# Attention weights transposed one query tile at a time, and a float32 value product in two column halves

## The chip, the cores and the metric

One core of a Trainium2 chip runs the whole program. The metric is device time in microseconds (us), the median of the runs of one kernel. TensorE (PE) multiplies matrices into PSUM; VectorE (DVE), ScalarE (ACT) and GpSimd (POOL) work on tiles; the DMA queues are fed by SyncE (SP). PEld stands for TensorE's weight loads, which can run beside its matmuls.

## The reference

A block of one layer on a sequence of 2048 rows with 1024 channels: RMS norm, one wide input projection, a state-space branch (SSD), a stick-breaking attention branch with 16 heads of 64 channels, gates, an output projection, and a norm. The part that the change touches is the attention:

```python
for blk in range(L // SB_BLOCK):
    ...
    logits = jnp.einsum('bqhd,bkhd->bhqk', q[:, q0:kend], k[:, :kend]).astype(jnp.float32) * scale
    mask = ki < qi
    log_fail = jnp.where(mask, jax.nn.log_sigmoid(-logits), 0.0)
    between = lax.cumsum(log_fail, axis=3, reverse=True) - log_fail
    w = jnp.where(mask, jnp.exp(jax.nn.log_sigmoid(logits) + between), 0.0)
    outs.append(jnp.einsum('bhqk,bkhd->bqhd', w.astype(v.dtype), v[:, :kend]))
```

## The kernel before, in words

The kernel runs in stages. First come the input projection's columns for the attention and the values (the V stage, `unit_v`), then the SSD branch (about 395 to 910 us), then the attention (about 929 to 2665 us), then the output.

Products with float32 accuracy are written in two ways. Most of them split each operand into a high and a low part of type fp32r, and add two or three fp32r products. Some are plain float32 products; each of these stands as two PE instructions in the trace. In the SSD stage the products `yp` are plain float32, with 64 columns of weights, and go by turns to the lower and the upper 64 partitions of one PSUM tile.

The attention works in steps `(h, qs, kc)`: a head, a block of 512 queries and a block of 512 keys, 160 steps in all. For each head, `qs` goes from 3 down to 0, and `kc` from `qs` down to 0. 64 of the steps are diagonal (`kc == qs`), 96 are not. A step has four query tiles `i` of 128 queries and four key blocks `kb` of 128 keys.

- `attn_qk(s, i)`: two products into `lg` (PE), two sigmoids into `tc` and `sw` (ACT), masks on POOL in diagonal steps, a running product over the keys (the scan, DVE), and the product of `sw` with it (DVE). The result `sw` holds the weights of query tile `i`: queries on partitions, keys along the row.
- `attn_tr(s, kb)`: the weights have to stand with the keys on partitions. For one key block it transposes the blocks of all query tiles `i` into one PSUM tile `wtp` (PE), and splits that into `wh` (ACT) and `wl` (DVE).
- `attn_av(s, kb)`: the product with the values of that key block. `vt` holds the high parts of the values in columns 0 to 63 and the low parts in columns 64 to 127; it is multiplied with `wh` and with `wl`, so `po` has the high parts' sum in one half of its partitions and the low parts' sum in the other, and the two are added at the end of a query block.

PE's order is written out by hand (`chain` ties each matmul to the one before it). The loop of a step goes over `i`: `attn_tr(s, i)`, `attn_qk(s + 1, i)`, `attn_av(s, i - 2)` from `i = 2` on, and `fill(i)`; then two more `attn_av` with a `fill` each. `fill` puts matmuls of other projections (`proj`) between, in shares given by `FW`. The other engines' queues follow the order in which a tile framework schedules the recorded operations.

Of the kernel before, what the change touches and what calls it, by code (L numbers as in the profile page):

```python
# [23 lines left out]
HD = 64  # L24
EPS = 1e-6
WARM = 24
FW = (0.8, 0.9, 1.0, 1.0, 1.1, 1.2)

COL_Z = 0
COL_X = 1024  # L30
# [18 lines left out]
def hybrid_kernel(ctx, tc, x, norm_pre, w_in, b_gate, conv_w, conv_b, dt_bias, a_log, d_skip,  # L49
# [57 lines left out]

    kst = [drp.tile([P, L], F32, name=f"kst{h}") for h in range(HEADS)]
    qst = [drp.tile([P, L], F32, name=f"qst{h}") for h in range(HEADS)]
    vst = [drp.tile([L, 4, P], F32, name=f"vst{i}") for i in range(HEADS // 4)]  # L110
    csd = drp.tile([HEADS, L], F32, name="csd")
    ytd = [drp.tile([D, TB], F32, name=f"ytd{t}") for t in range(NTB)]
    otd = [drp.tile([D, TB], F32, name=f"otd{t}") for t in range(NTB)]
# [272 lines left out]
    with tc.tile_pool(name="va", bufs=2) as va, tc.tile_pool(name="vp", bufs=2, space=PSUM) as vp:  # L386
        kn = va.tile([P, NCH, 16], F32, name="kn", bufs=1)

        def prep_v(i):
            c0, cw = vch[i]  # L390
            vh, vl = [], []
            for k in range(KT):
                raw = va.tile([P, cw], F32, name="vraw", tag="vraw", bufs=4)
                nc.sync.dma_start(raw, w_in[k * P:(k + 1) * P, c0:c0 + cw])
                h = va.tile([P, cw], F32R, name="vhi", tag="vhi", bufs=12)
                nc.scalar.copy(h, raw)
                l = va.tile([P, cw], F32R, name="vlo", tag="vlo", bufs=12)
                nc.vector.tensor_sub(l, raw, h.bitcast(F32))
                vh.append(h)
                vl.append(l)  # L400
            return vh, vl

        def unit_v(i, c, wv):
            c0, cw = vch[i]
            vh, vl = wv
            off = cw - VW
            tb, o = c // CPB, (c % CPB) * P
            ps = vp.tile([P, TB], F32, name="vps", tag="vps", bufs=3)
            for k in range(KT):
                xh, xl = hh[tb][:, k, o:o + P], hl[tb][:, k, o:o + P]  # L410
                matmul(ps[:, :cw], xh, vh[k], start=(k == 0), stop=False)
                yield
                matmul(ps[:, :cw], xh, vl[k], start=False, stop=False)
                yield
                matmul(ps[:, :cw], xl, vh[k], start=False, stop=(k == KT - 1))
                yield
            if off:
                nc.vector.tensor_copy(kn[:, c, :], ps[:, :16])
            v = va.tile([P, 4, 2, HD], F32R, name="vt", tag="vt", bufs=3)
            src = ps[:, off:cw].rearrange("p (h d) -> p h d", d=HD)  # L420
            nc.scalar.copy(v[:, :, 0, :], src)
            nc.vector.tensor_sub(v[:, :, 1, :], src, v[:, :, 0, :].bitcast(F32))
            nc.sync.dma_start(vst[i][c * P:(c + 1) * P], v.bitcast(F32).rearrange("p h s d -> p h (s d)"))

        def last_k():
            knf = kn.rearrange("p c d -> p (c d)")
            kd = kst[HEADS - 1].rearrange("(s d) t -> d s t", s=2)
            for r0 in range(0, NCH * 16, P):
                n = min(P, NCH * 16 - r0)
                tp = vp.tile([P, P], F32, name="ktp", tag="ktp")  # L430
                transpose(tp[:n], knf[:, r0:r0 + n], ident)
                kt = va.tile([P, 2, P], F32R, name="kt", tag="kt")
                nc.scalar.copy(kt[:n, 0, :], tp[:n])
                nc.vector.tensor_sub(kt[:n, 1, :], tp[:n], kt[:n, 0, :].bitcast(F32))
                for c in range(n // 16):
                    t0 = (r0 // 16 + c) * P
                    nc.sync.dma_start(kd[HD - 16:HD, :, t0:t0 + P], kt[c * 16:(c + 1) * 16].bitcast(F32))

        wv = prep_v(0)
        for tb in range(NTB):  # L440
            run(proj(w9, tb, done_qk(ev, 9, tb)))
        for i in range(len(vch)):
            for c in range(NCH):
                if c == max(0, NCH - 6) and i + 1 < len(vch):
                    nxt = prep_v(i + 1)
                run(unit_v(i, c, wv))
            if i == 0:
                later(20, last_k)
            if i + 1 < len(vch):
                wv = nxt  # L450
        wb = prep_a(COL_B)
        flush()
# [326 lines left out]

    steps = [(h, qs, kc) for h in range(HEADS) for qs in reversed(range(NTB)) for kc in reversed(range(qs + 1))]  # L780
    last_head = min(i for i, s in enumerate(steps) if s[0] == HEADS - 1)
    fills = {"gen": fill_h(), "left": n_main, "pos": 6 * last_head, "acc": 0.0, "late": False}

    def tick():
        clock[0] += 1
# [3 lines left out]
    def fill(i):  # L789
        f = fills  # L790
        if f["pos"] <= 0:
            for _ in f["gen"]:
                tick()
            if f["late"]:
                return
            f.update(gen=fill_y(box_y), left=8 * 24, pos=6 * (len(steps) - last_head) - 3, acc=0.0, late=True)
        f["acc"] += f["left"] / f["pos"] * FW[i]
        f["pos"] -= 1
        while f["acc"] >= 1.0:
            f["acc"] -= 1.0  # L800
            f["left"] -= 1
            if next(f["gen"], 0) == 0:
                f["left"] = 0
                break
            tick()
# [3 lines left out]
    def attn_load(s):  # L809
        if s >= len(steps):  # L810
            return
        h, qs, kc = steps[s]
        if (h, qs) not in qts:
            qa = ab.tile([P, TB], F32R, name="qa", tag="qa", bufs=2)
            qb = ab.tile([P, TB], F32R, name="qb", tag="qb", bufs=2)
            cols = slice(qs * TB, (qs + 1) * TB)
            nc.sync.dma_start(qa.bitcast(F32), qst[h][:, cols])
            nc.sync.dma_start(qb[0:HD].bitcast(F32), qst[h][HD:P, cols])
            nc.sync.dma_start(qb[HD:P].bitcast(F32), qst[h][0:HD, cols])
            qts[h, qs] = qa, qb  # L820
        if (h, kc) not in kts:
            k = ab.tile([P, TB], F32R, name="kt", tag="kt", bufs=4)
            nc.sync.dma_start(k.bitcast(F32), kst[h][:, kc * TB:(kc + 1) * TB])
            v = ab.tile([P, CPB, P], F32R, name="vt", tag="vt", bufs=4)
            nc.sync.dma_start(v.bitcast(F32), vst[h // 4][kc * TB:(kc + 1) * TB, h % 4, :].rearrange(
                "(c p) d -> p c d", p=P))
            kts[h, kc], vts[h, kc] = k, v

    def attn_qk(s, i):
# [29 lines left out]

    wts = {}  # L860

    def attn_tr(s, kb):
        h, qs, kc = steps[s]
        q0 = kb if kc == qs else 0
        lo = q0 * P
        tp = ap.tile([P, TB], F32, name="wtp", tag="wtp", bufs=3)
        for i in range(q0, CPB):
            transpose(tp[:, i * P:(i + 1) * P], ws[s, i][:, kb * P:(kb + 1) * P], ident)
        wh = ab.tile([P, TB], F32R, name="wh", tag="wh", bufs=3)
        nc.scalar.copy(wh[:, lo:], tp[:, lo:])  # L870
        wl = ab.tile([P, TB], F32R, name="wl", tag="wl", bufs=3)
        nc.vector.tensor_sub(wl[:, lo:], tp[:, lo:], wh[:, lo:].bitcast(F32))  # L872
        wts[s, kb] = lo, wh, wl

    def attn_av(s, kb):
        h, qs, kc = steps[s]
        lo, wh, wl = wts.pop((s, kb))
        if (h, qs) not in pos:
            pos[h, qs] = ap.tile([P, TB], F32, name="po", tag="po", bufs=1)
        po, v = pos[h, qs], vts[h, kc]  # L880
        first = kc == qs and kb == 0
        final = kc == 0 and kb == CPB - 1
        matmul(po[:, lo:], v[:, kb, :], wh[:, lo:], start=first, stop=False, skip_group_check=True)
        matmul(po[:, lo:], v[:, kb, :], wl[:, lo:], start=False, stop=final, skip_group_check=True)
        if final:
            e0 = (h % 2) * HD
            mine, other = slice(e0, e0 + HD), slice(HD - e0, P - e0)
            z = ab.tile([P, TB], F32, name="zl", tag="zl", bufs=1)
            nc.sync.dma_start(z[mine], zsd[qs][h * HD:(h + 1) * HD, :])
            o = gz.tile([P, TB], F32, name="o", tag="gz", bufs=2)  # L890
            nc.scalar.copy(o[mine], po[other])
            nc.vector.tensor_add(o[mine], o[mine], po[mine])  # L892
            nc.vector.tensor_mul(o[mine], o[mine], z[mine])  # L893
            nc.sync.dma_start(otd[qs][h * HD:(h + 1) * HD, :], o[mine])
# [9 lines left out]
    for s in range(len(steps)):  # L904
        attn_load(s + 2)
        for i in range(CPB):
            attn_tr(s, i)
            attn_qk(s + 1, i)
            if i >= 2:
                attn_av(s, i - 2)  # L910
            fill(i)
        for i in range(2, CPB):
            attn_av(s, i)
            fill(i + 2)
    for _ in fills["gen"]:
        pass
    close_ap()
# [150 lines left out]
```

## Time and profile before

| | |
|---|---|
| median of the runs | 3163.7 us (3163.27 to 3165.02, 3 runs) |
| the profiled execution's own time, its span | 3163.6 us |
| PE busy | 3024.1 us (96%) |
| DVE busy | 2457.2 us (78%) |
| ACT busy | 1585.7 us (50%) |
| POOL busy | 477.9 us (15%) |

The span is that of one profiled execution; nothing else lies around it here, and it agrees with the median. Matmuls are pipelined and their ends are modelled, so start times of neighbouring matmuls tell more than the durations: a 512-column fp32r matmul is shown with 0.39 us, while the next starts 0.23 us after it. An idle time in front of an instruction stands in brackets with what ended it.

### The profile page before, as it was taken

The numbers are of one execution on the slowest core, as the hardware profiler recorded it, in microseconds if no ns is written. First come the engines' busy times: TensorE is split into PE (matmuls) and PEld (weight loads), VectorE is DVE, ScalarE is ACT, GpSimd is POOL, SyncE is SP. The second block draws the span as 40 slices with busy tenths as digits, with TensorE's granted clock in tenths as the row PEclk, the third lists the DMA queues.
The fourth block names the chain that finished last, engine by engine and source line by source line (L and its number), as shares of the span: only waits on it lengthen the run. The fifth ranks groups of instructions, "written<-read, shape, count | busy, mean of one in ns | idle before, by whom it ended". The sixth has DMA issues, their size and how long they took to land.

```text
span 3163.6 us, 48155 instructions
## 1 busy us (share of the span) xinstructions
PE 3024.1 (96%) x16169; PEld 2496.9 (79%) x16169; DVE 2457.2 (78%) x4357; ACT 1585.7 (50%) x3102; POOL 477.9 (15%) x1626
## 2 busy tenths in 40 slices
PE   8999999999999999999999999999999989999998
PEld 6899888787877777777777777777777767888887
DVE  7321688768869989989899999989998899756553
ACT  6211345434446666566565666566665656333321
POOL 0000011100111212122212121222111231101000
PEclk9999999999999999999999999999999999999999
DMA  5532022212243334224323333334233334555452
GB/s 165 148 122 93 24 71 80 68 40 67 72 128 89 90 89 110 80 81 113 93 70 103 94 97 91 87 94 114 69 89 90 111 117 144 176 148 167 133 167 70
DMA packets 298816, 320.63 MB, mean 101 GB/s; under 512 B 23148, under 2 KB 187848, under 8 KB 298568
## 3 DMA queue, kind: packets, MB, share of 16 engines
q1 hardware_dynamic: 298416, 317.51, 34.6%
q8 instruction: 128, 2.10, 0.3%
q14 instruction: 120, 0.98, 0.1%
q10 hardware_dynamic: 152, 0.05, 0.0%
HBM read 216.67 MB, written 100.79 MB: 100 GB/s over the span
## 4 chain that ended last, share of the span: by engine, by line
PE 53%; DVE 33%; issue 5%; DMA 4%; ACT 4%; POOL 1%; SPq 0%; DVEq 0%; POOLq 0%; ACTq 0%
PE proj L74 30%; DVE tc L852 13%; PE po L74 8%; DVE sw L853 7%; PE vps L74 6%; DVE wl L872 5%; PE wtp L77 4%; PE lg L74 3%; DMA csb<-csd 2%; ACT sw L845 1%; ACT wh L870 1%; PE yp L74 1%; DVE acc L474 1%; DVE o L893 1%; DVE o L892 1%
## 5 line engine op out<-in xcount | busy, mean ns | idle before, releaser
L74 PE MATMUL proj<-hh,whi 128*128 128x512 f32 x1920 | 762.0, 397 | 0.1
L74 PE MATMUL proj<-hh,wlo 128*128 128x512 f32 x1920 | 761.7, 397 | 0.0
L74 PE MATMUL proj<-hl,whi 128*128 128x512 f32 x1920 | 760.4, 396 | 1.3 <-DVE hl L286 1.1
L870 ACT CAST wh<-wtp 128x512 fp32r<-128x512 f32 (+3 forms) x640 | 337.1, 527 | 390.2 <-PE wtp L77 386.6
L852 DVE TENSOR_TENSOR_SCAN tc<-tc,cy 128x513 f32<-128x513 f32 x384 | 490.9, 1278 | 0.3 <-ACT tc L843 0.3
L872 DVE TENSOR_TENSOR wl<-wtp,wh 128x512 fp32r<-128x512 f32 (+3 forms) x640 | 383.0, 599 | 81.5 <-ACT wh L870 80.3
L77 PE MATMUL wtp<-ident,sw 128*128 128x128 f32 x2176 | 369.9, 277 | 72.2 <-DVE sw L853 70.1
L853 DVE TENSOR_TENSOR sw<-sw,tc 128x512 f32<-128x512 f32 (+3 forms) x640 | 394.2, 616 | 50.5 <-POOL sw L849 13.5
L77 PEld LDWEIGHTS wtp<-ident,sw 128*128 128x128 f32 x2176 | 280.7, 141 | 181.0 <-DVE sw L853 99.1
L74 PEld LDWEIGHTS proj<-hl,whi 128*128 128x128 f32 x1920 | 362.6, 189 | 72.6 <-DVE hl L286 2.5
L74 PEld LDWEIGHTS proj<-hh,wlo 128*128 128x128 f32 x1920 | 362.6, 189 | 70.7 <-issue 0.3
L74 PEld LDWEIGHTS proj<-hh,whi 128*128 128x128 f32 x1920 | 362.7, 189 | 70.1 <-ACT hh L285 0.5
L845 ACT ACTIVATE sw<-lg 128x512 f32<-128x512 f32 (+3 forms) x640 | 346.1, 541 | 49.8 <-PE wtp L77 49.6
L843 ACT ACTIVATE tc<-lg 128x512 f32<-128x512 f32 (+3 forms) x640 | 349.1, 545 | 18.7 <-PE lg L74 13.1
L132 ACT CAST whi<-wraw 128x512 fp32r<-128x512 f32 x248 | 154.3, 624 | 280.5 <-PE proj L74 178.9
L74 PE MATMUL lg<-kt,qa 128*128 128x512 f32 (+3 forms) x640 | 285.1, 445 | 0.0
L74 PE MATMUL po<-wl,vt 128*128 128x512 f32 (+3 forms) x640 | 242.6, 379 | 29.0 <-DVE wl L872 28.2
L852 DVE TENSOR_TENSOR_SCAN tc<-tc 128x129 f32<-128x129 f32 (+3 forms) x256 | 218.1, 852 | 26.3 <-POOL tc L847 25.2
L74 PE MATMUL lg<-kt,qb 128*128 128x512 f32 (+3 forms) x640 | 234.6, 367 | 0.0
L74 PE MATMUL po<-wh,vt 128*128 128x512 f32 (+3 forms) x640 | 232.4, 363 | 0.0
L134 DVE TENSOR_TENSOR wlo<-wraw,whi 128x512 fp32r<-128x512 f32 x246 | 173.4, 706 | 73.3 <-ACT whi L132 70.5
L856 POOL COPY cy<-tc 128x1 f32<-128x1 f32 x384 | 133.6, 348 | 448.7 <-DVE tc L852 448.7
(202 smaller groups left out, 4887.8 us busy)
## 6 DMA issues: line engine op xcount, KB each, us to landing
wraw<-in_w_in SPq DMA_DIRECT2D x120, 256.0 KB, 3.0
vst<-vt SPq DMA_DIRECT2D x64, 256.0 KB, 2.0
csb<-csd SPq DMA_DIRECT2D x64, 256.0 KB, 4.4
qa<-qst SPq DMA_DIRECT2D x64, 256.0 KB, 3.5
qb<-qst SPq DMA_DIRECT2D x128, 128.0 KB, 3.8
kt<-kst SPq DMA_DIRECT2D x64, 256.0 KB, 3.2
vt<-vst SPq DMA_DIRECT2D x64, 256.0 KB, 3.0
gtd<-zb SPq DMA_DIRECT2D x64, 256.0 KB, 2.1
```

The lines of the kernel that those rows point to most:

```text
L74: chain(nc.tensor.matmul(*a, **k))
L77: chain(nc.tensor.transpose(*a))
L132: nc.scalar.copy(h, raw)
L134: (eng or nc.vector).tensor_tensor(l, raw, h.bitcast(F32), op=ALU.subtract)
L474: nc.vector.scalar_tensor_tensor(acc, xp[:, i:i + TB], pv[:, col:col + 1], acc, op0=ALU.mult, op1=ALU.add)
L843: nc.scalar.activation(t[:, :W], lg[:, :W], AF.Sigmoid, scale=-0.125)
L845: nc.scalar.activation(w[:, :W], lg[:, :W], AF.Sigmoid, scale=0.125)
L852: nc.vector.tensor_tensor_scan(tr, tr, tr, 1.0 if diag else carry[h, qs, i], ALU.mult, ALU.min)
L853: nc.vector.tensor_mul(w[:, :W], w[:, :W], t[:, 1:W + 1])
L856: nc.gpsimd.tensor_copy(c, t[:, 0:1])
L870: nc.scalar.copy(wh[:, lo:], tp[:, lo:])
L872: nc.vector.tensor_sub(wl[:, lo:], tp[:, lo:], wh[:, lo:].bitcast(F32))
```

## The change

`attn_tr` now takes a query tile `i` in place of a key block. It transposes that tile's four key blocks, and ACT copies them, undivided, as float32 into a buffer `wt` of the whole step (two such buffers). In a diagonal step only the blocks up to the diagonal are transposed, and POOL writes zeros into the one further block that the value product reads. `wl`, the DVE instruction for it, and the split of the values are gone: `vt` holds float32 values with 64 columns for each key block, in another layout in DRAM. `attn_av` works on a whole step: four plain float32 products with 64 columns of weights, the key blocks going by turns to the lower and the upper 64 partitions of `po`. It is issued once a step, for the step before (`attn_av(s - 1)`, after `attn_qk(s + 1, 1)` and `fill(1)`). `fill` has five places for a step in place of six.

```diff
--- before.py
+++ after.py
@@ -24,7 +24,7 @@
 HD = 64
 EPS = 1e-6
 WARM = 24
-FW = (0.8, 0.9, 1.0, 1.0, 1.1, 1.2)
+FW = (1.0, 1.0, 1.2, 1.2, 0.6)
 
 COL_Z = 0
 COL_X = 1024
@@ -107,7 +107,7 @@
 
     kst = [drp.tile([P, L], F32, name=f"kst{h}") for h in range(HEADS)]
     qst = [drp.tile([P, L], F32, name=f"qst{h}") for h in range(HEADS)]
-    vst = [drp.tile([L, 4, P], F32, name=f"vst{i}") for i in range(HEADS // 4)]
+    vst = [drp.tile([P, 4, NCH, HD], F32, name=f"vst{i}") for i in range(HEADS // 4)]
     csd = drp.tile([HEADS, L], F32, name="csd")
     ytd = [drp.tile([D, TB], F32, name=f"ytd{t}") for t in range(NTB)]
     otd = [drp.tile([D, TB], F32, name=f"otd{t}") for t in range(NTB)]
@@ -416,11 +416,9 @@
                 yield
             if off:
                 nc.vector.tensor_copy(kn[:, c, :], ps[:, :16])
-            v = va.tile([P, 4, 2, HD], F32R, name="vt", tag="vt", bufs=3)
-            src = ps[:, off:cw].rearrange("p (h d) -> p h d", d=HD)
-            nc.scalar.copy(v[:, :, 0, :], src)
-            nc.vector.tensor_sub(v[:, :, 1, :], src, v[:, :, 0, :].bitcast(F32))
-            nc.sync.dma_start(vst[i][c * P:(c + 1) * P], v.bitcast(F32).rearrange("p h s d -> p h (s d)"))
+            v = va.tile([P, 4, HD], F32, name="vt", tag="vt", bufs=3)
+            nc.scalar.copy(v, ps[:, off:cw].rearrange("p (h d) -> p h d", d=HD))
+            nc.sync.dma_start(vst[i][:, :, c, :], v)
 
         def last_k():
             knf = kn.rearrange("p c d -> p (c d)")
@@ -779,7 +777,7 @@
 
     steps = [(h, qs, kc) for h in range(HEADS) for qs in reversed(range(NTB)) for kc in reversed(range(qs + 1))]
     last_head = min(i for i, s in enumerate(steps) if s[0] == HEADS - 1)
-    fills = {"gen": fill_h(), "left": n_main, "pos": 6 * last_head, "acc": 0.0, "late": False}
+    fills = {"gen": fill_h(), "left": n_main, "pos": len(FW) * last_head, "acc": 0.0, "late": False}
 
     def tick():
         clock[0] += 1
@@ -793,7 +791,7 @@
                 tick()
             if f["late"]:
                 return
-            f.update(gen=fill_y(box_y), left=8 * 24, pos=6 * (len(steps) - last_head) - 3, acc=0.0, late=True)
+            f.update(gen=fill_y(box_y), left=8 * 24, pos=len(FW) * (len(steps) - last_head) - 3, acc=0.0, late=True)
         f["acc"] += f["left"] / f["pos"] * FW[i]
         f["pos"] -= 1
         while f["acc"] >= 1.0:
@@ -821,9 +819,8 @@
         if (h, kc) not in kts:
             k = ab.tile([P, TB], F32R, name="kt", tag="kt", bufs=4)
             nc.sync.dma_start(k.bitcast(F32), kst[h][:, kc * TB:(kc + 1) * TB])
-            v = ab.tile([P, CPB, P], F32R, name="vt", tag="vt", bufs=4)
-            nc.sync.dma_start(v.bitcast(F32), vst[h // 4][kc * TB:(kc + 1) * TB, h % 4, :].rearrange(
-                "(c p) d -> p c d", p=P))
+            v = ab.tile([P, CPB, HD], F32, name="vt", tag="vt", bufs=4)
+            nc.sync.dma_start(v, vst[h // 4][:, h % 4, kc * CPB:(kc + 1) * CPB, :])
             kts[h, kc], vts[h, kc] = k, v
 
     def attn_qk(s, i):
@@ -859,30 +856,31 @@
 
     wts = {}
 
-    def attn_tr(s, kb):
+    def attn_tr(s, i):
         h, qs, kc = steps[s]
-        q0 = kb if kc == qs else 0
-        lo = q0 * P
+        n = i + 1 if kc == qs else CPB
         tp = ap.tile([P, TB], F32, name="wtp", tag="wtp", bufs=3)
-        for i in range(q0, CPB):
-            transpose(tp[:, i * P:(i + 1) * P], ws[s, i][:, kb * P:(kb + 1) * P], ident)
-        wh = ab.tile([P, TB], F32R, name="wh", tag="wh", bufs=3)
-        nc.scalar.copy(wh[:, lo:], tp[:, lo:])
-        wl = ab.tile([P, TB], F32R, name="wl", tag="wl", bufs=3)
-        nc.vector.tensor_sub(wl[:, lo:], tp[:, lo:], wh[:, lo:].bitcast(F32))
-        wts[s, kb] = lo, wh, wl
-
-    def attn_av(s, kb):
+        sw = ws.pop((s, i))
+        for kb in range(n):
+            transpose(tp[:, kb * P:(kb + 1) * P], sw[:, kb * P:(kb + 1) * P], ident)
+        if i == 0:
+            wts[s] = ab.tile([P, CPB, TB], F32, name="wt", tag="wt", bufs=2)
+            if kc == qs:
+                nc.gpsimd.memset(wts[s][:, 1, 0:P], 0.0)
+        nc.scalar.copy(wts[s][:, 0:n, i * P:(i + 1) * P], tp[:, 0:n * P].rearrange("p (k q) -> p k q", q=P))
+
+    def attn_av(s):
         h, qs, kc = steps[s]
-        lo, wh, wl = wts.pop((s, kb))
         if (h, qs) not in pos:
             pos[h, qs] = ap.tile([P, TB], F32, name="po", tag="po", bufs=1)
         po, v = pos[h, qs], vts[h, kc]
-        first = kc == qs and kb == 0
-        final = kc == 0 and kb == CPB - 1
-        matmul(po[:, lo:], v[:, kb, :], wh[:, lo:], start=first, stop=False, skip_group_check=True)
-        matmul(po[:, lo:], v[:, kb, :], wl[:, lo:], start=False, stop=final, skip_group_check=True)
-        if final:
+        wt = wts.pop(s)
+        for kb in range(CPB):
+            lo = kb * P if kc == qs and kb > 1 else 0
+            e = (kb % 2) * HD
+            matmul(po[e:e + HD, lo:], v[:, kb, :], wt[:, kb, lo:], start=(kc == qs and kb < 2),
+                   stop=(kc == 0 and kb >= 2), skip_group_check=True)
+        if kc == 0:
             e0 = (h % 2) * HD
             mine, other = slice(e0, e0 + HD), slice(HD - e0, P - e0)
             z = ab.tile([P, TB], F32, name="zl", tag="zl", bufs=1)
@@ -906,12 +904,11 @@
         for i in range(CPB):
             attn_tr(s, i)
             attn_qk(s + 1, i)
-            if i >= 2:
-                attn_av(s, i - 2)
             fill(i)
-        for i in range(2, CPB):
-            attn_av(s, i)
-            fill(i + 2)
+            if i == 1 and s > 0:
+                attn_av(s - 1)
+                fill(CPB)
+    attn_av(len(steps) - 1)
     for _ in fills["gen"]:
         pass
     close_ap()
```

Three places in the program show what moves. The names are those of the tiles: `wtp` the transposed weights, `lg` the logits, `po` the value product, `proj` the filling projections; a trailing count stands for so many equal rows.

PE in the step in front of a diagonal one, before, from the transposes of key block 2 to those of key block 3:

```order
L77 MATMUL wtp<-ident,sw 128x128 x4
L74 MATMUL lg<-kt,qa 128x384
L74 MATMUL lg<-kt,qb 128x384
L74 MATMUL po<-wh,vt 128x512
L74 MATMUL po<-wl,vt 128x512
L74 MATMUL proj<-hh_195,wlo 128x512
L74 MATMUL proj<-hh_195,whi 128x512
L74 MATMUL proj<-hl_199,whi 128x512
L74 MATMUL proj<-hh_195,wlo 128x512
L77 MATMUL wtp<-ident,sw 128x128 x4
L74 MATMUL lg<-kt,qa 128x512
L74 MATMUL lg<-kt,qb 128x512
```

The same place in the changed kernel, from the transposes of query tile 1 to those of query tile 2:

```order
L77 MATMUL wtp<-ident,sw 128x128 x4
L74 MATMUL lg<-kt,qa 128x256
L74 MATMUL lg<-kt,qb 128x256
L74 MATMUL proj<-hh_197,whi 128x512
L74 MATMUL proj<-hl_201,whi 128x512
L74 MATMUL proj<-hh_197,wlo 128x512
L74 MATMUL proj<-hh_197,whi 128x512
L74 MATMUL po<-wt,vt 64x512 x4
L74 MATMUL proj<-hl_201,whi 128x512
L74 MATMUL proj<-hh_197,wlo 128x512
L74 MATMUL proj<-hh_197,whi 128x512
L77 MATMUL wtp<-ident,sw 128x128 x4
```

Before, a pair of `po` products with 512 columns follows each of the later `lg` pairs. Now four `po` products with 64 columns of weights stand together, once, behind the `proj` matmuls of the second query tile.

PE in a diagonal step, before; the rows start with the value product of key block 0:

```order
L74 MATMUL po<-wh,vt 128x512
L74 MATMUL po<-wl,vt 128x512
L74 MATMUL proj<-hh_196,whi 128x512
L74 MATMUL proj<-hl_200,whi 128x512
L74 MATMUL proj<-hh_196,wlo 128x512
L74 MATMUL proj<-hh_196,whi 128x512
L77 MATMUL wtp<-ident,sw 128x128
L74 MATMUL lg<-kt,qa 128x512
L74 MATMUL lg<-kt,qb 128x512
L74 MATMUL po<-wh,vt 128x384
L74 MATMUL po<-wl,vt 128x384
L74 MATMUL proj<-hl_200,whi 128x512
```

The value product of a diagonal step in the changed kernel (it stands inside the step after it), with its neighbours:

```order
L74 MATMUL proj<-hh_196,wlo 128x512
L74 MATMUL proj<-hh_196,whi 128x512
L74 MATMUL proj<-hl_200,whi 128x512
L74 MATMUL proj<-hh_196,wlo 128x512
L74 MATMUL po<-wt,vt 64x512 x2
L74 MATMUL po<-wt,vt 64x256
L74 MATMUL po<-wt,vt 64x128
L74 MATMUL proj<-hh_196,whi 128x512
L74 MATMUL proj<-hl_200,whi 128x512
L74 MATMUL proj<-hh_196,wlo 128x512
```

Before, four pairs with 512, 384, 256 and 128 columns are spread over the step. Now there are four products in a row, with 512, 512, 256 and 128 columns.

DVE at the same place, before; SCALAR_TENSOR_TENSOR with 129 to 513 columns is the scan:

```order
L852 SCALAR_TENSOR_TENSOR tc<-tc 128x129
L853 TENSOR_TENSOR sw<-sw,tc 128x128
L872 TENSOR_TENSOR wl<-wtp,wh 128x512
L852 SCALAR_TENSOR_TENSOR tc<-tc 128x257
L853 TENSOR_TENSOR sw<-sw,tc 128x256
L872 TENSOR_TENSOR wl<-wtp,wh 128x512
L852 SCALAR_TENSOR_TENSOR tc<-tc 128x385
L853 TENSOR_TENSOR sw<-sw,tc 128x384
L872 TENSOR_TENSOR wl<-wtp,wh 128x512
L852 SCALAR_TENSOR_TENSOR tc<-tc 128x513
```

DVE at the same place in the changed kernel:

```order
L849 SCALAR_TENSOR_TENSOR tc<-tc 128x129
L850 TENSOR_TENSOR sw<-sw,tc 128x128
L849 SCALAR_TENSOR_TENSOR tc<-tc 128x257
L850 TENSOR_TENSOR sw<-sw,tc 128x256
L849 SCALAR_TENSOR_TENSOR tc<-tc 128x385
L850 TENSOR_TENSOR sw<-sw,tc 128x384
L849 SCALAR_TENSOR_TENSOR tc<-tc 128x513
L850 TENSOR_TENSOR sw<-sw,tc 128x512
```

The `wl` rows between the scan and the product of one query tile and those of the next are gone; the rest keeps its order.

## Rows read from the trace of the kernel before

**Rows 1.** The page's first part: busy us (share of the span) and instructions.

```profile
PE 3024.1 (96%) x16169; PEld 2496.9 (79%) x16169; DVE 2457.2 (78%) x4357; ACT 1585.7 (50%) x3102; POOL 477.9 (15%) x1626
```

**Rows 2.** Windows: stretch, length, busy us (count) of PE, PEld, DVE, ACT, POOL, then PEclk, DMA.

```profile
200.00:400.00 200.00, 200.00 (x1398) 185.90 (x1397) 72.32 (x151) 44.54 (x91) 1.47 (x2) 1.00 0.20 70
929.00:2665.00 1736.00, 1629.86 (x8255) 1310.17 (x8254) 1580.38 (x2256) 1064.03 (x2235) 382.21 (x1548) 0.99 0.33 94
```

**Rows 3.** The chain that ended last, its shares of the span by engine.

```profile
PE 53%; DVE 33%; issue 5%; DMA 4%; ACT 4%; POOL 1%; SPq 0%; DVEq 0%; POOLq 0%; ACTq 0%
```

**Rows 4.** Who waited for whom, PE and PEld: us in total, times, longest.

```profile
PE wtp L77 <- DVE sw L853: 70.1, 92, 2.3
PE po L74 <- DVE wl L872: 28.2, 56, 2.1
PEld wtp L77 <- DVE sw L853: 99.1, 113, 2.5
PEld po L74 <- DVE wl L872: 59.1, 90, 2.3
```

**Rows 5.** Groups of instructions: busy us, mean ns, idle us before them, and what ended it.

```profile
L872 DVE TENSOR_TENSOR wl<-wtp,wh 128x512 fp32r<-128x512 f32 (+3 forms) x640 | 383.0, 599 | 81.5 <-ACT wh L870 80.3
L852 DVE TENSOR_TENSOR_SCAN tc<-tc,cy 128x513 f32<-128x513 f32 x384 | 490.9, 1278 | 0.3 <-ACT tc L843 0.3
L853 DVE TENSOR_TENSOR sw<-sw,tc 128x512 f32<-128x512 f32 x448 | 310.6, 693 | 21.9 <-ACT tc L843 0.5
L845 ACT ACTIVATE sw<-lg 128x512 f32<-128x512 f32 x448 | 271.3, 606 | 23.7 <-PE wtp L77 23.6
```

**Rows 6.** Timeline of PE around two attention steps: start us, us, instruction, idle before.

```profile
1521.47 0.22 PE L74 MATMUL po<-wh,vt 128*128 128x128 f32 x1
1522.12 0.33 PE L74 MATMUL po<-wl,vt 128*128 128x128 f32 x1 [0.43 <-DVE wl L872]
...
1523.50 0.49 PE L77 MATMUL wtp<-ident,sw 128*128 128x128 f32 x3
1524.72 0.33 PE L77 MATMUL wtp<-ident,sw 128*128 128x128 f32 x1 [0.73 <-DVE sw L853]
...
1532.01 0.40 PE L74 MATMUL po<-wh,vt 128*128 128x512 f32 x1
1532.24 0.40 PE L74 MATMUL po<-wl,vt 128*128 128x512 f32 x1
1532.47 0.39 PE L74 MATMUL proj<-hl,whi 128*128 128x512 f32 x1
```

**Rows 7.** Timeline of PE around one group of yp products in the SSD stage.

```profile
623.59 0.39 PE L74 MATMUL proj<-hl,whi 128*128 128x512 f32 x1
623.91 0.44 PE L74 MATMUL yp<-dl,xd 128*64 128x128 f32 x4
624.18 0.39 PE L74 MATMUL yp<-csb,S 128*64 128x128 f32 x4
...
625.49 0.39 PE L74 MATMUL yp<-csb,S 128*64 128x128 f32 x4
625.81 0.50 PE L74 MATMUL proj<-hh,wlo 128*128 128x512 f32 x1
626.14 0.39 PE L74 MATMUL proj<-hh,whi 128*128 128x512 f32 x1
```

**Rows 8.** Timeline of PE at a float32 product over all 128 columns.

```profile
365.95 1.05 PE L74 MATMUL scp<-cT,bT 128*128 128x128 f32 x8
366.76 0.48 PE L74 MATMUL proj<-hl,whi 128*128 128x512 f32 x1
```

**Rows 9.** The weight loads of the yp products, same columns as rows 5.

```profile
L74 PEld LDWEIGHTS yp<-dl,xd 128*64 128x64 f32 x512 | 32.8, 136 | 11.3 <-issue 10.2 <-DVE S L540 0.7 <-PE proj L74 0.4
```

**Rows 10.** The page's DMA issues: count, KB each, us to landing.

```profile
vt<-vst SPq DMA_DIRECT2D x64, 256.0 KB, 3.0
```


## Prediction

> **What bounds the kernel now.** I read the page's first part first: PE is busy 96% of the span, DVE 78% [rows 1]. That share is an average, so the windows come next. In 200 to 400 us, into which the projection of the values reaches, PE has no idle time at all; in the attention, 929 to 2665 us, it is busy 1629.9 of 1736 us and DVE 1580.4 [rows 2]. So 106.1 us of PE are idle there, and two engines are close to full. The chain that ended last says which of them holds the other up: 53% of it lies on PE and 33% on DVE [rows 3]. The list of waits gives the places: PE's transposes wait 70.1 us for `sw`, and the value product 28.2 us for `wl`, both from DVE [rows 4]; these 98.3 us are nearly all of the 106.1.
>
> The reason is in the order of a step. The transposes of key block 0 need `sw` of all four query tiles, the last of which is made at the end of the step before. DVE is late with it: off the diagonal a step asks it for 4 x (1.278 + 0.693) = 7.9 us of scans and products, and 383.0 / 160 = 2.4 us of `wl` [rows 5], 10.3 us in a step that lasts 1736 / 160 = 10.85 us on average. Then `wl` stands in the same queue, and the value product waits for it. A smaller loop lies on ACT: `sw` cannot be written while its buffer still awaits the transposes of key block 3 (23.6 us of ACT's idle time [rows 5]).
>
> **The change part by part.** The sum is made against the profiled execution's own 3163.6 us, which is within 0.1 us of the median.
>
> Waits removed. A query tile's transposes now need only its own `sw`, whose logits PE issued a whole step earlier; the way from there through ACT, the scan and the product is 0.606 x 2 + 1.278 + 0.693 = 3.2 us without queueing, against more than 10 us. DVE loses the 383.0 us of `wl`; 1580.4 - 383.0 = 1197 us are left for a stage of some 1670 us, 72%. So I expect both waits nearly gone. Their price is more than the idle time shown, because a stop also delays the next start: the `po` matmul of 128 columns at 1521.47 should be followed after a quarter of 0.23 us, that is 0.06, and is followed after 0.65 us; 0.59 us are lost where 0.43 are shown. For the transposes, three from 1523.50 at 0.10 each (the pace of [rows 8]) would let the fourth start at 1523.80; it starts at 1524.72, 0.92 lost for 0.73 shown [rows 6]. With 0.17 more for each of 148 waits, 98.3 becomes 123. The weight loads show 99.1 + 59.1 = 158 us [rows 4], short waits included; the bounds are 98 and 158, and I take 130, nearer the matmuls' own rows.
>
> The value product on PE, before: a 512-column product starts 0.23 us after the last one [rows 6]. Off the diagonal there are 8, 1.84 us; on it 2 x (512 + 384 + 256 + 128) columns are worth five, 1.15 us.
>
> The value product, after: plain float32 with 64 weight columns in alternating halves. This trace has the same form in `yp`: a row "x4" is two products of 128 columns (each shows as two instructions), and six such rows from 624.18 to 625.49 take 0.218 us each [rows 7]. A float32 product on all 128 columns takes 0.81 / 4 = 0.20 us [rows 8]. So two products in opposite halves cost what one costs: they run side by side. At 512 columns a pair is 4 x 0.218 = 0.87 us. Off the diagonal: two pairs, 1.74 us. On it: one pair at 512 and one at 256 (its partner of 128 lies beside it), 1.31 us.
>
> Going in and out of the half-array form also costs. From [rows 7]: into the group 0.32 where 0.23 is usual, the first row 0.27 for 0.218, out of it 0.32 for 0.218, the next `proj` 0.33 for 0.23; together 0.09 + 0.05 + 0.10 + 0.10 = 0.34 us, call it 0.35. Each of the 160 steps has one group, with `proj` on both sides, so all of it counts: 56 us. Lower bound zero, if the 512-column stream hides it; the upper bound is twice it.
>
> PE's price: 96 x (1.74 - 1.84 + 0.35) + 64 x (1.31 - 1.15 + 0.35) = 24 + 33 = 57 us. Alone, the edit of the product makes PE slower; the gain comes from the waits.
>
> Edits priced at nothing. The transposes and the ACT copies keep their number and sizes. `attn_av` one step later gives ACT's copies more than half a step, and `po` is needed again only a step after its last sum. POOL's 64 zero blocks stand in a queue that is busy 382 of 1736 us [rows 2]; they wait for a `wt` buffer that the value product gave back half a step before. If that cover were gone, the value product would wait, and behind it all of PE. The final addition into `o` now waits on DVE for a product that ends later; what is queued behind it is the scan and product of query tiles 2 and 3, which have most of a step to spare. The loads of `vt` halve from 256 KB landing in 3.0 us [rows 10], and SP issues them two steps ahead. The V stage loses its DVE splits, which held PE up in no way (its 200.00 busy of 200), and its stores become smaller pieces, first read hundreds of us later.
>
> Left over: 10 us of waits that I cannot place, for steps in which other DVE work falls together; bounds 0 and 40.
>
> Sum: 3163.6 - 130 + 57 + 10 = 3100.6, so 3100 us.
>
> **The rivals.**
> 1. Cheaper passage: the loads' 158 us were the true price, and of the 0.35 us only 0.1 remains at 512 columns. The price on PE is then 17 us (zero off the diagonal, 0.26 on it): 3163.6 - 158 + 17 + 5 = 3028; either part alone gives 3060 to 3072. For it: the long stream gives time to hide a load. Against: the 0.10 us behind the last pair is a drain, and a longer stream drains no sooner.
> 2. The change does not do what it says, and half the waits stay: the value product is now one block of some 2.1 us on PE, so the logits arrive at DVE in bursts, with `o` waiting in its queue for that block. 3163.6 - 65 + 57 = 3156. It decides if DVE is more than half a step behind; its 72% speaks against it.
> 3. Weight loads in the open: 8 loads, in pairs, of 136 ns [rows 9], each pair standing between two pairs of matmuls: 160 x 4 x 0.136 = 87 us more, 3187, slower. Against it stands the 0.218 us for two such pairs, in which a pair of loads already lies [rows 7]; it decides if pairs of 512 columns start over 0.5 us apart. The Trainium skill, "TensorE: Matmul & The Clock Gate", in the section on what overlaps and what doesn't, says that a weight load runs beside matmuls in flight only where its row group differs; here both halves use all rows, so by that rule this rival would hold. The trace disagrees, by the same 0.218 us.
> 4. No side by side at 512 columns: the sum grows by 96 x 1.74 + 64 x 1.31 = 251 us, 3351, slower. [Rows 7] speak against it; those products have 128 columns, though, and these up to 512.
>
> **How the numbers follow.** The forecast has 0.62, with a range of its own from 3075 to 3130; rival 1 has 0.15, rival 2 0.12, rival 3 0.06, rival 4 0.05. From 3050 to 3155 lie the forecast, more than half of rival 1 and nearly half of rival 2: about 0.8 with what may go wrong inside the forecast. A measurement of this kernel tells 0.2%, 6 us, from no change. Faster: the forecast, rival 1 and two thirds of rival 2, 0.85. Same: the rest of rival 2, 0.04. Slower: rivals 3 and 4, 0.11.
>
> **What would show it.** In the attention of the changed kernel: PE's waits for `sw` under 20 us, DVE near 72% busy, and no wait of `po` for DVE. A `po` group: pairs 0.43 us apart, a diagonal group 1.3 us and any other 1.7 us long, and around it 0.32 us where 0.23 is usual. The stage should end near 2600 us, with all before 929 us unmoved. Waits for `sw` over 60 us would show rival 2; pairs over 0.5 us apart rival 3; single starts 0.43 us apart with 8 to a group rival 4; and a stage that grows shorter while PE's price is below 30 us rival 1.

## The result and the profile after

The changed kernel takes 3057.2 us (median; 3055.6 to 3058.7), the kernel before 3163.6 on the same chip: a ratio of 0.966, interval 0.9647 to 0.9675. That is 106 us less, inside the range given (3050 to 3155), but 43 us below the forecast of 3100. The profiled execution is 3055.6 us long, 108.0 less than before.

The last addition into `o` ends the attention. Its row in the list of the tile `po`, of the kernel before and then of the changed one (count, ns least/median/most, first and last start in us):

```profile
L892 DVE TENSOR_TENSOR o<-o,po x64: 667/686/693, 981.2 to 2664.6; 64x512 f32<-64x512 f32 x64
```

```profile
L890 DVE TENSOR_TENSOR o<-o,po x64: 669/686/693, 976.8 to 2556.8; 64x512 f32<-64x512 f32 x64
```

107.8 of the 108.0 us lie ahead of that point, and the projection of the values, whose DVE splits went, gave nothing: the window from 200 to 400 us is as full as before (below, against [rows 2]). The first logits mark the start of the attention, before and then after:

```profile
L74 PE MATMUL lg<-kt,qa x640: 220/476/776, 929.1 to 2649.9; 128*128 128x512 f32 x96, 128*128 128x128 f32 x64
```

```profile
L74 PE MATMUL lg<-kt,qa x640: 220/476/775, 925.2 to 2545.1; 128*128 128x512 f32 x96, 128*128 128x128 f32 x64
```

So some 4 us of the gain lie ahead of the attention (this start differs by as much between the versions below), and 104 us are the attention's own.

The page of the changed kernel, its first line and the chain's shares:

```profile
PE 3012.0 (99%) x16169; PEld 2342.6 (77%) x16169; DVE 2140.1 (70%) x3653; ACT 1585.5 (52%) x3102; POOL 505.3 (17%) x1690
...
PE 88%; DVE 7%; DMA 3%; issue 1%; ACT 0%; POOL 0%; SPq 0%; ACTq 0%; DVEq 0%; POOLq 0%
```

Two of its windows, with the columns of [rows 2]:

```profile
929.00:2560.00 1631.00, 1617.89 (x8246) 1155.12 (x8245) 1290.34 (x1615) 1062.99 (x2231) 407.68 (x1605) 1.00 0.34 95
200.00:400.00 200.00, 200.00 (x1396) 185.81 (x1396) 55.49 (x110) 44.63 (x91) 1.85 (x2) 1.00 0.17 42
```

PE now has 13.1 us idle in the attention where it had 106.1 [rows 2], and the chain lies on PE for 88% in place of 53%, on DVE for 7% in place of 33% [rows 3]. The lists of waits of PE and of its weight loads show what is left of [rows 4]:

```profile
PE lg L74 <- ACT sw L842: 2.5, 2, 1.6
PE po L74 <- ACT wt L870: 1.7, 2, 1.0
...
PEld po L74 <- issue: 139.1, 449, 0.6
PEld proj L74 <- issue: 101.2, 160, 0.8
```

Of the four waits of [rows 4] none is left. The new rows on "issue" name no other engine: the weight loads stand still inside each group of the half-array product and at the first `proj` behind it, 160 times in the second row, once a step. The groups of instructions (columns as in [rows 5]) show what became of ACT and DVE:

```profile
L849 DVE TENSOR_TENSOR_SCAN tc<-tc,cy 128x513 f32<-128x513 f32 x384 | 491.7, 1281 | 56.0 <-ACT tc L840 52.3
L850 DVE TENSOR_TENSOR sw<-sw,tc 128x512 f32<-128x512 f32 (+3 forms) x640 | 400.8, 626 | 74.6 <-POOL cy L853 1.4
L842 ACT ACTIVATE sw<-lg 128x512 f32<-128x512 f32 (+3 forms) x640 | 344.8, 539 | 0.0
```

The scan, which hardly ever waited (0.3 us), now waits for ACT: DVE is the engine that is early. ACT's own loop over the `sw` buffers is gone (0.0 us). The value product on PE, in the timeline, off the diagonal and on it:

```profile
1506.00 0.40 PE L74 MATMUL proj<-hh,whi 128*128 128x512 f32 x1
1506.33 1.94 PE L74 MATMUL po<-wt,vt 128*64 128x512 f32 x8
1508.19 0.50 PE L74 MATMUL proj<-hl,whi 128*128 128x512 f32 x1
1508.53 0.39 PE L74 MATMUL proj<-hh,wlo 128*128 128x512 f32 x1
...
1515.97 0.39 PE L74 MATMUL proj<-hh,whi 128*128 128x512 f32 x1
1516.29 1.50 PE L74 MATMUL po<-wt,vt 128*64 128x512 f32 x8
1517.73 0.50 PE L74 MATMUL proj<-hl,whi 128*128 128x512 f32 x1
1518.07 0.40 PE L74 MATMUL proj<-hh,wlo 128*128 128x512 f32 x1
```

From the `proj` in front to the second one behind, 2.53 and 2.10 us; less 2 x 0.23 for the two `proj`, a group costs 2.07 and 1.64 us, passage in and out included. Before, the same count has to be made at a pair that nothing stops. The shortest one, of 128 columns:

```profile
1447.39 0.39 PE L74 MATMUL proj<-hl,whi 128*128 128x512 f32 x1
1447.62 0.22 PE L74 MATMUL po<-wh,vt 128*128 128x128 f32 x1
1447.68 0.28 PE L74 MATMUL po<-wl,vt 128*128 128x128 f32 x1
1447.79 0.45 PE L74 MATMUL proj<-hh,wlo 128*128 128x512 f32 x1
1448.08 0.40 PE L74 MATMUL proj<-hh,whi 128*128 128x512 f32 x1
```

0.69 us less 0.46 is 0.23, twice the 0.115 that its share of the columns would give. Over the undisturbed pairs of that trace a diagonal step's value product comes to 1.26 us, where the prediction worked out 1.15, and any other step's to 1.86. So the new product costs 96 x 0.21 + 64 x 0.38 = 44 us more, and the waits that went were worth 104 + 44 = 148 us, net of the 4 us of new ones in the first two of the lines on waits above. Counted directly, from each start on PE to the next one, the transposes took 95 us longer before than in the changed kernel and the value products 54 us longer than undisturbed ones, 149 in all.

### The profile page after: what moved, and what is told of

It is laid out like the page before. It is cut to its first block, busy times and chain, and to the rows that moved or that the text cites. A ratio compares the mean times of both kernels' runs of the same rounds, so it can differ in the third digit from the quotient of the medians.

```text
span 3055.6 us, 47953 instructions
## 1 busy us (share of the span) xinstructions
PE 3012.0 (99%) x16169; PEld 2342.6 (77%) x16169; DVE 2140.1 (70%) x3653; ACT 1585.5 (52%) x3102; POOL 505.3 (17%) x1690
## 4 chain that ended last, share of the span: by engine, by line
PE 88%; DVE 7%; DMA 3%; issue 1%; ACT 0%; POOL 0%; SPq 0%; ACTq 0%; DVEq 0%; POOLq 0%
PE proj L74 49%; PE po L74 14%; PE lg L74 8%; PE wtp L77 8%; PE vps L74 6%; DMA csb<-csd 3%; DVE acc L472 1%; PE yp L74 1%; DVE S L538 1%; DVE csb L520 1%; DVE dl L518 1%; DVE dl L514 1%; PE stp L74 0%; DMA xt<-in_x 0%; DVE wlo L134 0%
## 5 line engine op out<-in xcount | busy, mean ns | idle before, releaser
L870 ACT COPY wt<-wtp 128x512 f32<-128x512 f32 (+3 forms) x640 | 336.4, 526 | 396.2 <-PE wtp L77 374.5
L850 DVE TENSOR_TENSOR sw<-sw,tc 128x512 f32<-128x512 f32 (+3 forms) x640 | 400.8, 626 | 74.6 <-POOL cy L853 1.4
L77 PE MATMUL wtp<-ident,sw 128*128 128x128 f32 x2176 | 341.7, 272 | 0.0
L74 PE MATMUL po<-wt,vt 128*64 128x512 f32 (+2 forms) x1280 | 283.5, 554 | 1.7 <-ACT wt L870 1.7
L74 PEld LDWEIGHTS po<-wt,vt 128*64 128x64 f32 x1280 | 77.9, 136 | 151.9 <-issue 139.1
L504 POOL TENSOR_TENSOR xe<-xd,dec 128x512 f32<-128x512 f32 x32 | 49.8, 1556 | 829.5 <-DVE xd L502 829.5
L839 POOL MEMSET tc<- 128x1 f32 x640 | 62.6, 98 | 739.5 <-DVE sw L850 720.0
```

What stands on the lines that cost most here:

```text
L74: chain(nc.tensor.matmul(*a, **k))
L77: chain(nc.tensor.transpose(*a))
L504: nc.gpsimd.tensor_tensor(heads(xe), heads(xd), tok(dec), op=ALU.mult)
L839: nc.gpsimd.memset(t[:, W:W + 1], 1.0)
L850: nc.vector.tensor_mul(w[:, :W], w[:, :W], t[:, 1:W + 1])
L870: nc.scalar.copy(wts[s][:, 0:n, i * P:(i + 1) * P], tp[:, 0:n * P].rearrange("p (k q) -> p k q", q=P))
```

## The experiments

The prediction left two things open: which part of the change frees PE, and what a stop of PE really costs. Theory A: the order does it, since a query tile's transposes need only their own `sw`. Theory B: the relief of DVE does it. The runs e1 to e4 were made on one chip, e5 to e8 on a second and e9 on a third, each beside the kernel before, which took 3163.4 to 3163.9 us on all three. The intervals are of 95%.

| kernel | us | ratio to before, interval |
|---|---|---|
| e1, split kept, order by query tile | 3163.8 | 0.9998, 0.9988 to 1.0007 |
| e2, value product at the end of its own step | 3047.6 | 0.9634, 0.9617 to 0.9650 |
| e3, transposes by key block | 3480.6 | 1.0996, 1.0979 to 1.1012 |
| e4, all four products in one half | 3269.1 | 1.0328, 1.0312 to 1.0343 |
| e5, by key block, product at the end | 3106.4 | 0.9818, 0.9805 to 0.9832 |
| e6, product behind transposes | 3056.8 | 0.9663, 0.9650 to 0.9677 |
| e7, products of two steps in a group | 3030.9 | 0.9580, 0.9567 to 0.9593 |
| e8, two query tiles together | 3037.0 | 0.9598, 0.9585 to 0.9611 |
| e9, e7 and e8 | 3022.5 | 0.9556, 0.9543 to 0.9569 |

**e1: the order without the relief.** The split, its DVE instruction and eight fp32r products come back, in the order by query tile. The high and the low parts have one buffer of a step each, and the product stands at the end of its own step. The edit, shortened:

```diff
-        nc.scalar.copy(wts[s][:, 0:n, i * P:(i + 1) * P], tp[:, 0:n * P].rearrange("p (k q) -> p k q", q=P))
+        nc.scalar.copy(wh, tq)
+        nc.vector.tensor_sub(wl, tq, wh.bitcast(F32))
...
+        fill(CPB)
+        attn_av(s)
```

> Transposes by query tile into a buffer of the step, but the high and low parts and their DVE instruction stay, with eight fp32r products at the end of the step (a second buffer for the next step does not fit beside the first). Theory A, the order frees PE: the waits for sw stay gone although DVE has its 383 us back, and PE saves the 53 us that the float32 product costs: about 3010 us. Theory B, the relief of DVE frees PE: DVE is again asked for 10.3 us in a step off the diagonal, the waits come back at that engine, 3100 to 3160 us.

3163.8 us, no gain at all. Its waits, of PE and of the loads:

```profile
PE po L74 <- DVE wl L875: 115.1, 101, 3.9
...
PEld po L74 <- DVE wl L875: 167.6, 125, 4.2
```

Its window over the attention:

```profile
929.00:2664.00 1735.00, 1613.02 (x8259) 1310.62 (x8258) 1586.13 (x2258) 1062.65 (x2236) 379.62 (x1548) 0.99 0.33 94
```

Theory A in its pure form falls. The wait for `sw` is gone, as A said, but DVE is as full as before (1586 of 1735 us) and PE waits for `wl` in its place: the order only moved the stop from the transposes to the value product. Whether the order would pay without the relief if the product came a step later, so that `wl` had more time, no run shows; the buffers for that do not fit.

**e2: the later issue undone.**

```diff
             fill(i)
-            if i == 1 and s > 0:
-                attn_av(s - 1)
-                fill(CPB)
-    attn_av(len(steps) - 1)
+        fill(CPB)
+        attn_av(s)
```

> The changed kernel, with the value product at the end of its own step (behind the last two fills) in place of one step later. Theories A and B alike: the last copy needs 0.6 us on ACT, the logits and fills in front of the product take over 2 us, so 3057 us within 6. If the later issue carries the gain, PE waits for the copy in 160 steps, 0.3 to 1 us each: 3100 to 3200 us.

3047.6 us: 10 us less than the changed kernel and a little below the band expected; the two intervals just touch. The later issue carries none of the gain. Part of the 10 us is the neighbour: behind the group stand transposes here, and from their first start to the logits it takes 0.41 us where 0.35 is usual (0.06 more), against 0.11 more for `proj` in the changed kernel, 160 times.

**e3: the relief without the order.** The edit, shortened; ACT copies whole key blocks accordingly.

```diff
-    def attn_tr(s, i):
+    def attn_tr(s, kb):
...
-        for kb in range(n):
-            transpose(tp[:, kb * P:(kb + 1) * P], sw[:, kb * P:(kb + 1) * P], ident)
+        for i in range(q0, CPB):
+            transpose(tp[:, i * P:(i + 1) * P], ws[s, i][:, kb * P:(kb + 1) * P], ident)
```

> The changed kernel, with the transposes by key block as before (float32 product, buffer of the step and later issue stay; DVE has no split). Theory A, the order: the first transposes of a step wait for the last sw again, 70 to 100 us of waits: 3130 to 3160 us. Theory B, the relief: DVE is 72% busy and in time, 3057 to 3070 us.

3480.6 us, far outside what either theory gave. The sum of PE's waits for `sw`:

```profile
PE wtp L77 <- DVE sw L850: 287.0, 164, 3.1
```

The timeline of PE at one of them:

```profile
1648.12 0.49 PE L77 MATMUL wtp<-ident,sw 128*128 128x128 f32 x3
1650.79 0.47 PE L77 MATMUL wtp<-ident,sw 128*128 128x128 f32 x1 [2.17 <-DVE sw L850]
1650.91 0.77 PE L74 MATMUL lg<-kt,qa 128*128 128x512 f32 x1
...
1652.34 0.63 PE L74 MATMUL proj<-hh,wlo 128*128 128x512 f32 x1
1652.77 0.63 PE L74 MATMUL proj<-hh,whi 128*128 128x512 f32 x1
```

The window around it, with the granted clock third from the end:

```profile
1650.00:1654.00 4.00, 3.21 (x9) 2.53 (x10) 2.51 (x3) 1.67 (x3) 0.28 (x2) 0.58 0.25 68
```

The kernel takes away a cover as well: between the last logits of a step and the first transposes of the next there is one `fill` left; the value product and the other `fill` stand at the second tile. PE waits 2.17 us there, and then the granted clock is 0.58 over the four us of the window, with `proj` starts 0.43 us apart in place of 0.23: mostly the lower of the two levels, 1.2 and 2.4 GHz. So e3 prices a lost cover, and not the order; e5 gives the cover back.

**e5: by key block, with the cover of before.** e3 and e2's edit together: the value product and both fills stand at the end of the step.

> Transposes by key block, float32 product at the end of its own step, behind the last two fills: between the last logits of a step and the first transposes of the next lie again some 3.8 us of PE work, as in the kernel before, against 3.2 us from the logits to the finished weights. If the relief of DVE alone is enough where that cover stands (and the 3481 us of the run by key block came from the cover that was taken away), the waits for sw are small: 3050 to 3075 us. If the order by query tile is needed in itself, the waits of 70 to 160 us are back: 3120 to 3210 us.

3106.4 us, between the two expectations. PE's waits and the loads' waits for `sw`:

```profile
PE wtp L77 <- DVE sw L850: 47.4, 56, 3.3
...
PEld wtp L77 <- DVE sw L850: 67.0, 73, 3.5
```

Between e5 and e2 there is only the order: 58.7 us. So the relief alone brings 57 us net of the product's price, the order on top of it 59 us more, and the order without the relief, in the form of e1, nothing.

**e4: the halves not side by side.** The edit, shortened; the rest fits the start and stop flags and the last addition to it and leaves out the zero block.

```diff
-            e = (kb % 2) * HD
+            e = 0
```

> The changed kernel, with all four float32 products in the lower half of the partitions, one after another (diagonal steps without the zero block). If two products in opposite halves run side by side at 512 columns: off the diagonal 3.49 us for 1.74, on it 2.18 for 1.31, 96 x 1.75 + 64 x 0.87 = 224 us more, about 3280 us. If the halves bring nothing: 3057 us.

3269.1 us, 212 more than the changed kernel, where 224 were expected. The timeline of PE at a diagonal group:

```profile
1503.55 0.40 PE L74 MATMUL proj<-hh,whi 128*128 128x512 f32 x1
1503.88 2.37 PE L74 MATMUL po<-wt,vt 128*64 128x512 f32 x8
1506.17 0.50 PE L74 MATMUL proj<-hl,whi 128*128 128x512 f32 x1
```

2.29 us from start to start, against 1.44 (1516.29 to 1517.73) with the halves by turns. The side-by-side run is worth more than the whole gain: with the products in one half, the kernel would have become slower than before.

**e6: the product between transposes and logits.**

```diff
             attn_tr(s, i)
+            if i == 1 and s > 0:
+                attn_av(s - 1)
             attn_qk(s + 1, i)
             fill(i)
             if i == 1 and s > 0:
-                attn_av(s - 1)
                 fill(CPB)
```

> The changed kernel, with the value product between the transposes and the logits of the second query tile, no proj matmul beside it. Each change from float32 to fp32r products costs some 0.09 us in front of the logits anyway. If the passage into and out of the half-array product is a cost of changing form, it falls together with that one: 160 x 0.1 = 10 to 16 us less than 3057. If it is a drain of the group alone, whatever stands beside it: 3057 within 5.

3056.8 us, the same. Its timeline at one group:

```profile
1504.34 0.38 PE L77 MATMUL wtp<-ident,sw 128*128 128x128 f32 x2
1504.65 1.94 PE L74 MATMUL po<-wt,vt 128*64 128x512 f32 x8
1506.52 0.50 PE L74 MATMUL lg<-kt,qa 128*128 128x512 f32 x1
1506.86 0.39 PE L74 MATMUL lg<-kt,qb 128*128 128x512 f32 x1
```

Two transposes at 0.11 and then 0.09 more before the group: the passage in costs the same behind float32 transposes as behind `proj`, and the passage out (0.34 for 0.23, at the first logits) the same as well. The 0.09 us that the expectation puts in front of the logits anyway are no cost, as the rows of e8 below show; so there was nothing for the passage to merge with.

**e7, e8 and e9: fewer changes of form.** e7 puts the value products of two steps of a query block together, e8 the transposes and then the logits of two query tiles, both on e2.

```diff
-        attn_av(s)
+        late.append(s)
+        if len(late) == 2 or steps[s][2] == 0:
+            while late:
+                attn_av(late.pop(0))
```

```diff
-        for i in range(CPB):
-            attn_tr(s, i)
-            attn_qk(s + 1, i)
-            fill(i)
+        for i in range(0, CPB, 2):
+            for j in (i, i + 1):
+                attn_tr(s, j)
+            for j in (i, i + 1):
+                attn_qk(s + 1, j)
+            for j in (i, i + 1):
+                fill(j)
```

> The value products of two steps of one query block in one group at the end of the second step: 96 groups in place of 160, beside the run with the product at the end of each step (3048 us). If each group costs its passage, 0.29 us in that place: 64 x 0.29 = 19 us less, 3029. If the longer block makes the logits late for ACT and DVE: 3048 or more.

> The value product at the end of its step, and the transposes of two query tiles together, then the logits of the two: half of the passages from float32 transposes to fp32r logits, which show 0.316 us where 0.23 is usual. If that is a cost of each passage: 320 x 0.087 = 28 us less than 3048, 3020. If it is only a start shown late: 3048 within 5; if the logits in pairs make PE wait for an lg buffer: more than 3055.

> The two edits of the runs before together: value products of two steps in one group, transposes and logits of two query tiles together. If the two gains add up (17 us for the group of two steps, 11 us for the two tiles, both against 3048): 3020 us. If the longer stretches without logits make ACT and DVE late, the sum is not reached: 3031 or more.

e7 takes 3030.9 us, 17 less than e2, where 64 passages of 0.29 us were expected to give 19. A group of it:

```profile
1511.61 0.40 PE L74 MATMUL proj<-hl,whi 128*128 128x512 f32 x1
1511.94 3.22 PE L74 MATMUL po<-wt,vt 128*64 128x512 f32 x16
1515.09 0.33 PE L77 MATMUL wtp<-ident,sw 128*128 128x128 f32 x1
```

Sixteen instructions stand between one passage in and one out. e8 takes 3037.0 us, 11 less than e2, where 28 were expected. One query tile of the changed kernel, and then two together in e8, from the first transpose to the first `proj` behind the logits:

```profile
1510.95 0.60 PE L77 MATMUL wtp<-ident,sw 128*128 128x128 f32 x4
1511.30 0.48 PE L74 MATMUL lg<-kt,qa 128*128 128x512 f32 x1
1511.62 0.39 PE L74 MATMUL lg<-kt,qb 128*128 128x512 f32 x1
1511.85 0.39 PE L74 MATMUL proj<-hh,whi 128*128 128x512 f32 x1
```

```profile
1542.04 1.03 PE L77 MATMUL wtp<-ident,sw 128*128 128x128 f32 x8
...
1543.84 0.39 PE L74 MATMUL proj<-hl,whi 128*128 128x512 f32 x1
```

0.90 us for one tile, 1.80 for two: half as many changes of form save nothing here. The 0.32 us behind the first logits, where 0.23 is usual, is only a start shown early: four transposes at 0.11 (128 columns of float32, 0.218 / 2 in [rows 7]) and two logits at 0.23 make the 0.90. So e8's 11 us are not the passage that it was built to remove. Counted from start to start, they lie in the `proj` matmuls, which hold 829 us of the attention in e2 and 815 in e8; why was not tried. Both together take 3022.5 us where the sum of the two gives 3020, the fastest version here: 35 us less than the changed kernel.

## Why the prediction was right, and where it was off

**What bounds the kernel: right.** DVE held PE up; e1 and e5 show that the relief is needed, and that it is not all. The prediction priced the waits for `sw` and `wl` as one sum and named the relief of DVE and the order by query tile side by side as what removes them; the runs part the two: relief 57 us net, order 59 more, order alone (as in e1) nothing.

**The price of the waits: too small.** "I take 130, nearer the matmuls' own rows" is the term that was mis-sized, with the 10 us "left over" behind it: 120 us net, where the runs show 148. That is 28 of the 45 us between the sum, 3100.6, and the profiled 3055.6; 13 lie in the price of the value product, and 4 ahead of the attention. The loads' rows were nearer: 158 us [rows 4]. Two more pairs of runs say the same. From e5 to e2: 58.7 us of time, 67.0 on the loads' rows, 47.4 on PE's. From e1 to e2: 116 us and some 38 that the float32 product costs in e2's place, 154 in all; 167.6 on the loads' rows, 115.1 on PE's. PE's rows count a stop from where the modelled end of the last matmul lies, and so lose part of it, as in the prediction's two stops (0.59 for 0.43 shown, 0.92 for 0.73). A small part of the 148 is clock: the mean granted clock is 0.993 before and 0.995 after, 22 and 15 us of full speed lost, 7 us apart.

**The value product on PE: right in form, a little dear.** 2.09 and 1.66 us a group were worked out from the `yp` rows, 2.07 and 1.64 measured; the passage of 0.35 us, read there too, shows as 0.33: 0.10 in front, 0.11 behind, and the rest inside the group. What was too small is the diagonal step of before, 1.15 us by its columns and 1.26 measured. So 57 us were worked out and 44 measured.

**Edits priced at nothing: right.** The window of the values' projection is as full as before, no `vt` load or POOL write shows up among PE's waits, and the later issue of the value product can be undone without loss (e2).

**DVE's share: a little off.** 72% was worked out, 1290 of 1631 us, 79%, measured: DVE's rows overlap their neighbours (before, they add up to 1705 us in 1580 busy ones), so taking out 383.0 us of them takes 290 from the time in which it is busy. The forecast's sum did not use it; the chance of rival 2 did.

**The rivals.** Rival 1 was half right: the loads' 158 us were near the true price, but the passage was not cheaper. Rival 2 (half of the waits stay) did not hold: none of the four waits is left; e5, with the old order, keeps some of them. Rivals 3 and 4 are excluded: a diagonal group of 1.44 us holds eight loads of 136 ns without showing them, and e4 shows what the serial form costs. The rule of the Trainium skill, "TensorE: Matmul & The Clock Gate", in the section on what overlaps and what doesn't, that a weight load runs beside matmuls only where its row group differs, would make rival 3 hold; the trace disagrees, by the same 1.44 us.

## What to carry to other kernels

Price a stop of TensorE by the idle time of its weight loads rather than by that of its matmuls; in three pairs of runs of this kernel the loads were 7 to 14% too high and the matmuls 19 to 34% too low. Look for a product of the wanted form elsewhere in the same trace: the SSD stage's `yp` gave a group of the new value product as 2.09 us where 2.07 were measured. The price of the old form has to be read at rows that nothing stops, the short ones too; the share of the columns gave 1.15 us for 1.26. And when a nearly full engine holds up another, ask first what work can be taken off it: in e1 a better order behind a DVE that was as full as before only moved the wait.

## What was not expected

A stop can cost twice. In e3, PE waits 2.17 us for one transpose, and the granted clock is 0.58 from 1650 to 1654 us; over the run the mean is 0.968 where the changed kernel has 0.995, some 96 us of full speed more lost. The run is 423 us longer than the changed kernel, while PE's waits for `sw` show 287.0 us. The weight loads' waits for it show more:

```profile
PEld wtp L77 <- DVE sw L850: 340.6, 182, 3.3
```

With the 96 us of clock that makes 437 us, near the 423. e5, with the same order of transposes and the cover given back, has 0.994. So work that only fills a gap can hold the clock up.

The 0.32 us in front of the second logits looked like a cost of going from float32 transposes to fp32r logits; two runs (e6 and e8) were planned on it. Adding up the starts across the whole stretch, as above for e8, would have shown beforehand that nothing is lost there. What made the `proj` matmuls of e8 cheaper stays open.
